# Feed-forward gate and up products by Strassen's algorithm in a hybrid encoder trunk on one Trainium2 core

## Chip, cores and metric

One core of one Trainium2 chip runs the whole step as one program. The metric is device time in microseconds from one launch; the number of a kernel is the median of its runs. The kernel before has 2403.69 us (three runs, 2400.80 to 2404.43).

## The reference, cut to what matters

The program computes two layers of a streaming encoder for 512 prompt tokens and 8 x 16 sample tokens, 640 columns in all, width 1024, in fp32. Each layer has a mixer (pooling and differential attention in layer 0, RWKV-7 in layer 1), a cross-attention and a SwiGLU feed-forward of width 2816. What the change touches is the last of these:

```python
D_FF = -(-8 * D_MODEL // (3 * 256)) * 256        # 2816 = 22 blocks of 128
def swiglu(h, wg, wu, wd):
    return (jax.nn.silu(h @ wg) * (h @ wu)) @ wd
...
        h = rmsnorm(x, P['norm_ffn_g'][l])
        x = x + swiglu(h, P['ffn_wg'][l], P['ffn_wu'][l], P['ffn_wd'][l])
```

## The kernel before, in words

Activations lie with features on the 128 partitions and the 640 tokens along the row; x is 8 such blocks. TensorE multiplies in a rounded fp32 format. To keep fp32 accuracy every operand is split (`split`, L216): the high part is a cast on ScalarE (L220), the low part the difference to it on VectorE (L211, or L214 when a scale is applied). A product is the sum of three: high by high, weight high by input low, weight low by input high. Weights come by `load_w` (L238): one DMA on SP's queue into `wr` (L245), a cast into `wh` on ScalarE (L247), a subtraction into `wl` on VectorE. `wtile` (L233) hands out two buffers each of wr, wh and wl in turn.

`block_steps` (L257) multiplies one block of 128 outputs: for each of the 8 blocks k of the inputs, the three products, each for two halves of 320 columns (`HALVES`), into two PSUM banks that take turns; 48 matmuls (L230) for a block of 1024 inputs. `gemm` (L274) strings such blocks together, with an evacuation function for each.

`ffn` (L1036), called once for each layer after `cross`, works so. `normed` (L523) multiplies x by the norm's gain and splits it into `xn`, without the row scale. `rms` (L484) works out the row scale: Square on ScalarE, the sum over the eight blocks in `acc` (GpSimd, the last one VectorE), a matmul with ones, root, reciprocal, a diagonal matrix, again a matmul with ones into `rstd`. Gate and up are computed in three groups of 8, 8 and 6 hidden blocks f. For each f the gate block is multiplied by rstd (VectorE) and goes through Silu (ScalarE); the up block is multiplied by rstd (VectorE), then by the gate (GpSimd), and split into `hid`. After each group the output projection adds 8 blocks to x (`add_x`, L530). Six PSUM banks serve these products in turn, two the norm. At the last group of layer 0, `mem_parts` transposes the memory prompt for the next layer through the banks of role r.

The order of instructions on each engine is worked out when the program is built: instructions are placed by their order in the program and by a simulated time at which they can run, so that later work may be placed ahead of earlier work that would still wait. On the chip every engine then keeps that order.

`cross` (L903) ends with a product of 8 blocks (24 matmuls each) that adds to x; `rwkv` (L1072) follows layer 0's feed-forward, `final` (L1895) layer 1's. SBUF holds 56 slots of 656 columns (`t`), 22 half slots of 256 (`n`, `NHALF`), and some wide tiles (zr0, zr1, bk0, bk1) that `rwkv` uses.

Of the kernel before, what the change touches and what calls it, by code (L numbers as in the profile page):

```python
# [9 lines left out]
F32 = mybir.dt.float32  # L10
F32R = mybir.dt.float32r
AF = mybir.ActivationFunctionType
ALU = mybir.AluOpType
# [8 lines left out]
NT = NP + NB * TS  # L22
NF = 22
HALVES = ((0, 320), (320, 320))
NEG = -1.0e30
EPS = 1e-6
NSLOT = 56
NHALF = 22
NSMALL = 32


# [8 lines left out]
class Trunk:  # L40
# [21 lines left out]
    def __init__(self, ctx, tc, io):  # L62
# [5 lines left out]
        self.dr = ctx.enter_context(tc.tile_pool(name="dr", bufs=1, space=DRAM))  # L68
        self.free = {"t": deque(range(NSLOT)), "n": deque(range(NHALF))}
        self.scopes = [{}]  # L70
# [54 lines left out]
    def take(self, k, name, kind="t", dt=F32):  # L125
        h = Held()
        h.slots = [(kind, self.pop(kind, name)) for _ in range(k)]
        h.extend(self.slot(kind, i, name, dt) for _, i in h.slots)
        return h
# [102 lines left out]

    def wtile(self, kind, dt):  # L233
        i = self.turn[kind]
        self.turn[kind] = (i + 1) % 2
        return self.wp.tile([128, 1024], dt, tag=f"{kind}{i}", name=kind, bufs=1)

    def load_w(self, src, kb, cols, rows=128):  # L238
# [795 lines left out]


    def ffn(self, l):  # L1036
        nc, io = self.nc, self.io
        self.banks(g=(0, 1, 2, 3, 4, 5), r=(6, 7))
        wg, wu, wd = io["ffn_wg"][l], io["ffn_wu"][l], io["ffn_wd"][l]
        hl = self.normed(self.col["norm_ffn_g"][:, 8 * l:8 * l + 8])  # L1040
        first = [[self.load_w(self.wview(w, 0, 8, 0, 128), 8, 128)] for w in (wg, wu)]
        _, rstd = self.rms("r")
        r0 = rstd[0]
        for f0, nf in ((0, 8), (8, 8), (16, 6)):
            hid = self.hl(nf, "hid")
            with self.scope():
                for f in range(nf):
                    g = self.t("gate")[:, 0:NT]
                    sg = self.t("sgate")[:, 0:NT]

                    def ev_g(m, pts):
                        for p, (t0, n) in zip(pts, HALVES):
                            self.tt(g[:, t0:t0 + n], p, r0[:, t0:t0 + n])
                            self.act(sg[:, t0:t0 + n], g[:, t0:t0 + n], AF.Silu)

                    def ev_u(m, pts):
                        for p, (t0, n) in zip(pts, HALVES):
                            self.tt(g[:, t0:t0 + n], p, r0[:, t0:t0 + n])
                            self.tt(g[:, t0:t0 + n], g[:, t0:t0 + n], sg[:, t0:t0 + n], eng=nc.gpsimd)
                            self.split((hid[f][0][:, t0:t0 + n], hid[f][1][:, t0:t0 + n]), g[:, t0:t0 + n])  # L1060

                    self.gemm(hl, wg, 128, ev_g, c0=(f0 + f) * 128, first=() if f0 + f else first[0])
                    self.gemm(hl, wu, 128, ev_u, c0=(f0 + f) * 128, first=() if f0 + f else first[1])
            if f0 == 16:
                self.give(hl, rstd)
                if l == 0:
                    self.mem = self.mem_parts("r")
            self.gemm(hid, wd, 1024, self.add_x, r0=f0 * 128)
            self.give(hid)


    def rwkv(self):  # L1072
# [898 lines left out]
```

## Time and profile before

| | |
|---|---|
| median of three runs | 2403.69 us (2400.80 to 2404.43) |
| profiled execution, its own time | 2400.51 us |
| its span, first to last instruction | 2398.7 us |
| TensorE busy | 2258.0 us (94%), 19213 matmuls, mean granted clock 0.967 |
| VectorE, ScalarE, GpSimd busy | 1257.2, 821.4, 448.3 us |
| DMA | 280.45 MB, mean 117 GB/s |

The span is the time between the first and the last instruction; the execution's own time is 1.8 us longer. Matmuls overlap, so the mean of one (310 ns) is longer than the distance from one to the next. A row of idle time names the engine whose event ended it. The granted clock is given as a share of 2.4 GHz; 0.5 is the lower level, 1.2 GHz.

### The profile page before, as it was taken

The numbers are of one execution on the slowest core, as the hardware profiler recorded it, in microseconds if no ns is written. First come the engines' busy times: TensorE is split into PE (matmuls) and PEld (weight loads), VectorE is DVE, ScalarE is ACT, GpSimd is POOL, SyncE is SP. The second block draws the span as 40 slices with busy tenths as digits, with TensorE's granted clock in tenths as the row PEclk, the third lists the DMA queues.
The fourth block names the chain that finished last, engine by engine and source line by source line (L and its number), as shares of the span: only waits on it lengthen the run. The fifth ranks groups of instructions, "written<-read, shape, count | busy, mean of one in ns | idle before, by whom it ended". The sixth has DMA issues, their size and how long they took to land. (4 is left out here: it accounts for less than half of the span.)

```text
span 2398.7 us, 46090 instructions
## 1 busy us (share of the span) xinstructions
PE 2258.0 (94%) x19213; PEld 2109.6 (88%) x19213; DVE 1257.2 (52%) x2193; ACT 821.4 (34%) x1521; POOL 448.3 (19%) x476
## 2 busy tenths in 40 slices
PE   8998899999999999989998976898999999999998
PEld 7886799879999999988887875676998899999997
DVE  3467434445433434485758885588534544244344
ACT  4335332334222212366745431222323432122122
POOL 1113220002101101245433111132100211021010
PEclk9999999999999999999998887898999999999998
DMA  3228545533222222353235666573444222222222
GB/s 118 75 71 304 155 136 158 172 93 89 80 71 80 71 85 74 112 171 107 83 111 160 164 166 165 165 223 111 145 128 154 69 76 72 80 71 80 80 73 77
DMA packets 428194, 280.45 MB, mean 117 GB/s; under 512 B 79001, under 2 KB 383406, under 8 KB 427985
## 3 DMA queue, kind: packets, MB, share of 16 engines
q1 hardware_dynamic: 424385, 268.01, 38.2%
q0 software_dynamic: 3600, 9.49, 1.1%
q8 instruction: 151, 2.47, 0.4%
q14 instruction: 58, 0.48, 0.1%
HBM read 231.22 MB, written 46.20 MB: 116 GB/s over the span
## 5 line engine op out<-in xcount | busy, mean ns | idle before, releaser
L230 PE MATMUL p_g<-xn,wh 128*128 128x320 f32 x3712 | 720.3, 310 | 0.4 <-ACT wh L247 0.4
L230 PEld LDWEIGHTS p_g<-xn,wh 128*128 128x128 f32 x3712 | 588.9, 188 | 9.6 <-issue 8.4
L247 ACT CAST wh<-wr 128x1024 fp32r<-128x1024 f32 (+3 forms) x287 | 274.4, 957 | 851.7 <-PE p_g L230 548.1
L230 PE MATMUL p_g<-xn,wl 128*128 128x320 f32 x1856 | 443.1, 310 | 3.6 <-DVE wl L211 3.6
L211 DVE TENSOR_TENSOR wl<-wr,wh 128x1024 fp32r<-128x1024 f32 (+2 forms) x259 | 307.3, 1186 | 71.6 <-ACT wh L247 59.6
L230 PEld LDWEIGHTS p_g<-xn,wl 128*128 128x128 f32 x1856 | 315.4, 188 | 7.5 <-DVE wl L211 4.0
L230 PE MATMUL p_g<-hid,wh 128*128 128x320 f32 x1408 | 264.4, 309 | 0.0
L211 POOL TENSOR_TENSOR gate<-gate,sgate 128x320 f32<-128x320 f32 x88 | 118.0, 1362 | 727.5 <-DVE gate L211 727.5
L211 DVE TENSOR_TENSOR gate<-p_g,rstd 128x320 f32<-128x320 f32 x176 | 78.4, 486 | 326.9 <-PE p_g L230 324.3
L211 DVE TENSOR_TENSOR x<-x,p_g 128x320 f32<-128x320 f32 x208 | 93.1, 484 | 266.4 <-PE p_g L230 266.3
L230 PEld LDWEIGHTS p_g<-hid,wh 128*128 128x128 f32 x1408 | 220.8, 188 | 0.0
L230 PE MATMUL p_g<-hid,wl 128*128 128x320 f32 x704 | 160.8, 309 | 0.0
L230 PE MATMUL p_g<-mixr,wh 128*128 128x320 f32 (+2 forms) x640 | 131.8, 317 | 5.9 <-ACT wh L247 1.8
L230 PEld LDWEIGHTS p_g<-hid,wl 128*128 128x128 f32 x704 | 117.8, 188 | 0.0
L230 PEld LDWEIGHTS p_g<-mixr,wh 128*128 128x128 f32 (+2 forms) x640 | 100.4, 182 | 15.8 <-issue 5.9
L230 PE MATMUL p_g<-xohl,wh 128*128 128x320 f32 x512 | 110.0, 319 | 3.7 <-ACT xohl L220 3.6
L230 PEld LDWEIGHTS p_g<-xohl,wh 128*128 128x128 f32 x512 | 82.3, 188 | 8.8 <-ACT xohl L220 5.9
L211 POOL TENSOR_TENSOR acc<-acc,sq 128x640 f32<-128x640 f32 x30 | 51.8, 1726 | 164.4 <-ACT sq L208 164.4
L230 PE MATMUL p_g<-mixr,wl 128*128 128x320 f32 (+2 forms) x320 | 79.2, 316 | 0.0
L211 POOL TENSOR_TENSOR wl<-wr,wh 128x1024 fp32r<-128x1024 f32 (+2 forms) x28 | 65.4, 2340 | 70.2 <-ACT wh L247 68.9
L211 DVE TENSOR_TENSOR hid<-gate,hid 128x320 fp32r<-128x320 f32 x88 | 71.5, 812 | 9.0 <-ACT hid L220 9.0
L972 POOL TENSOR_SCALAR xp<-xp,xsm 128x256 f32<-128x256 f32 x32 | 15.3, 478 | 311.6 <-DVE xsm L708 299.6
(491 smaller groups left out, 3719.5 us busy)
## 6 DMA issues: line engine op xcount, KB each, us to landing
wr<-in_ffn_wg SPq DMA_DIRECT2D x44, 512.0 KB
wr<-in_ffn_wu SPq DMA_DIRECT2D x44, 512.0 KB
kc<-in_cache_mem_k SPq DMA_DIRECT2D x64, 256.0 KB
vc<-in_cache_mem_v SPq DMA_DIRECT2D x64, 256.0 KB
wr<-in_ffn_wd SPq DMA_DIRECT2D x32, 512.0 KB
wr<-in_ev_w_in SPq DMA_DIRECT2D x16, 512.0 KB
wr<-in_xa_wk SPq DMA_DIRECT2D x16, 512.0 KB
vc<-in_cache_diff_v SPq DMA_DIRECT2D x32, 256.0 KB
```

Of the source, the lines that this page charges most:

```text
L211: (eng or self.nc.vector).tensor_tensor(out, a, b, op=op)
L230: self.nc.tensor.matmul(out, lhsT, rhs, start=start, stop=stop, **kw)
L247: nc.scalar.copy(wh[0:rows, 0:n], wr[0:rows, 0:n])
L972: nc.gpsimd.tensor_scalar(p, p, rs, 1.0, op0=ALU.mult, op1=ALU.mult)
```

## The change

Hidden blocks 0 to 3 of the 22 stay plain products; the other 18 are taken in nine pairs. For a pair (f, f+1) gate and up weights are cut into four parts: A11 and A12 are f by inputs 0 to 3 and 4 to 7, A21 and A22 the same of f+1; a tile holds the gate part in its first 512 columns and the up part in the other 512. The inputs are cut the same way into B11, B12, B21, B22 (inputs 0 to 3 or 4 to 7, columns 0 to 319 or 320 to 639). Strassen's algorithm (in Winograd's form) makes the 2 x 2 product with seven products of parts: four sums of weights (S1, S2, and in place A11-A21, A12-S2) on VectorE for each pair, four sums of inputs (T1 to T4) once a layer, and sums of the products in PSUM or by VectorE after ScalarE has copied a partial sum out.

For that the inputs are normalized before they are split: `rms` runs first, `ys` = x times gain times rstd, and `xn` is split from it. The product with rstd after the matmuls goes away, and Silu reads PSUM. The gate product moves from GpSimd to VectorE. The groups are of 4, 6, 6 and 6 blocks. `wh` and `wl` get three buffers, for all weight loads of the kernel; `NHALF` goes from 22 to 14 for their room. The raw weight parts lie in the four wide tiles and the two wr buffers and change places from pair to pair (`at`).

```diff
-NHALF = 22
+NHALF = 14
@@ wtile
-        self.turn[kind] = (i + 1) % 2
+        self.turn[kind] = (i + 1) % (2 if kind == "wr" else 3)
@@ ffn
-        hl = self.normed(self.col["norm_ffn_g"][:, 8 * l:8 * l + 8])
+        gcol = self.col["norm_ffn_g"][:, 8 * l:8 * l + 8]
         first = [[self.load_w(self.wview(w, 0, 8, 0, 128), 8, 128)] for w in (wg, wu)]
         _, rstd = self.rms("r")
-        r0 = rstd[0]
-        for f0, nf in ((0, 8), (8, 8), (16, 6)):
+        ys = self.blocks(8, "xf")
+        hl = self.hl(8, "xn")
+        for k in range(8):
+            self.stt(ys[k], self.x[k], gcol[:, k:k + 1], rstd[0])
+            self.split(hl[k], ys[k])
+        L, R = slice(0, 320), slice(320, 640)
+        c, d = self.hl(4, "xc"), self.hl(2, "xd")
+            hid = self.hl(4, "hid")
+            for f in range(4):
+                def ev_g(m, pts):
+                    for p, (t0, n) in zip(pts, HALVES):
+                        self.act(sg[:, t0:t0 + n], p, AF.Silu)
+                def ev_u(m, pts):
+                    for p, (t0, n) in zip(pts, HALVES):
+                        self.tt(pr[:, t0:t0 + n], p, sg[:, t0:t0 + n])
+                    self.split(hid[f], pr)
+                self.gemm(hl, wg, 128, ev_g, c0=f * 128, first=() if f else first[0])
+                self.gemm(hl, wu, 128, ev_u, c0=f * 128, first=() if f else first[1])
+                if f == 1:
+                    for k in range(4):
+                        y1, y2 = ys[k], ys[4 + k]
+                        self.tt(y1[:, L], y1[:, R], y1[:, L], ALU.subtract)
+                        self.tt(y1[:, R], y2[:, R], y1[:, R], ALU.subtract)
+                        self.tt(y2[:, R], y2[:, R], y1[:, L], ALU.subtract)
+                        self.tt(y2[:, L], y2[:, L], y2[:, R], ALU.subtract)
+                        self.split(c[k], y2)
+                        self.split([t[:, (L, R)[k % 2]] for t in d[k // 2]], y1[:, R])
+        for k in range(4):
+            self.split((hl[k][0][:, R], hl[k][1][:, R]), ys[k][:, L])
+        self.gemm(hid, wd, 1024, self.add_x)
...
+        for f0, nf in ((4, 6), (10, 6), (16, 6)):
+            self.banks(a=(0, 1, 2, 3), b=(4, 5, 6, 7), g=(4, 5, 6, 7), r=(6, 7))
+            hid = self.hl(nf, "hid")
+            at = dict(A11=0, A21=1, A22=2, A12=3, S1=4, S2=5)
+                for f in range(0, nf, 2):
+                    self.strassen(wg, wu, f0 + f, rhs, hid[f:f + 2], at)
+                    at = dict(A21=at["A11"], A22=at["S2"], A11=at["S1"], A12=at["A21"], S1=at["A12"], S2=at["A22"])
...
             self.gemm(hid, wd, 1024, self.add_x, r0=f0 * 128)
@@ strassen, new
+        for nm, fi, kh in (("A21", 1, 0), ("A22", 1, 1), ("A11", 0, 0), ("A12", 0, 1)):
+            A[nm] = raw(nm)
+            for i, w in enumerate((wg, wu)):
+                nc.sync.dma_start(out=A[nm][:, 512 * i:512 * i + 512].rearrange("p (k m) -> p k m", k=4),
+                                  in_=self.wview(w, 512 * kh, 4, (f + fi) * 128, 128))
+        def parts(t):
+            hi, lo = self.wtile("wh", F32R), self.wtile("wl", F32R)
+            self.split((hi, lo), t)
+            return [w.rearrange("p (i k m) -> p i k m", i=2, k=4) for w in (hi, lo)]
+        def product(pts, w, x, start):
+            for i, p in enumerate(pts):
+                n = 0
+                for k in range(4):
+                    for a, b in ((0, 0), (0, 1), (1, 0)):
+                        self.mm(p[:, 0:320], w[a][:, i, k, :], rhs[x][k][b], start=start and n == 0, stop=n == 11, skip_group_check=True)
+                        n += 1
+        def take(pts, i, s):
+            for p, t in zip(pts, tmp[i]):
+                nc.scalar.copy(t[:, s], p[:, 0:320])
+        def out(i, s, pts=None, direct=False):
+            tg, tu = [t[:, s] for t in tmp[i]]
+            if direct:
+                self.act(tg, pts[0][:, 0:320], AF.Silu)
+                self.tt(pr[i][:, s], pts[1][:, 0:320], tg)
+                return
+            self.tt(tg, tg, pts[0][:, 0:320], ALU.add)
+            self.act(tg, tg, AF.Silu)
+            self.tt(tu, tu, pts[1][:, 0:320], ALU.add)
+            self.tt(pr[i][:, s], tu, tg)
+        S1, S2 = raw("S1"), raw("S2")
+        self.tt(S1, A["A21"], A["A22"], ALU.add)
+        self.tt(S2, S1, A["A11"], ALU.subtract)
+        self.tt(A["A21"], A["A11"], A["A21"], ALU.subtract)
+        pa = [self.ps("a") for _ in range(2)]
+        product(pa, parts(A["A11"]), "B11", True)
+        take(pa, 0, L)
+        pb = [self.ps("b") for _ in range(2)]
+        product(pb, parts(A["A12"]), "B21", True)
+        out(0, L, pb)
+        product(pa, parts(S2), "T2", False)
+        take(pa, 1, L)
+        self.tt(A["A12"], A["A12"], S2, ALU.subtract)
+        product(pa, parts(S1), "T1", False)
+        take(pa, 1, R)
+        pc = [self.ps("b") for _ in range(2)]
+        product(pc, parts(A["A21"]), "T3", True)
+        out(1, R, pc)
+        product(pa, parts(A["A12"]), "B22", False)
+        out(0, R, pa, True)
+        self.split(hid[0], pr[0])
+        product(pc, parts(A["A22"]), "T4", False)
+        out(1, L, pc)
+        self.split(hid[1], pr[1])
```

## Rows read from the trace of the kernel before

**Rows 1.** The page's first part: busy time of each engine, its share of the span, and its instructions.

```profile
PE 2258.0 (94%) x19213; PEld 2109.6 (88%) x19213; DVE 1257.2 (52%) x2193; ACT 821.4 (34%) x1521; POOL 448.3 (19%) x476
```

**Rows 2.** The windows view over the feed-forward of layer 0 and of layer 1. Columns: the stretch, its length, busy time and instructions of PE, PEld, DVE, ACT and POOL, granted TensorE clock, busy share of DMA, GB/s.

```profile
560.35:1027.40 467.05, 467.05 (x3200) 466.69 (x3199) 190.03 (x261) 118.54 (x178) 70.55 (x59) 1.00 0.28 83
1914.74:2380.50 465.76, 465.76 (x3184) 465.44 (x3183) 186.16 (x252) 109.71 (x161) 60.07 (x45) 1.00 0.26 74
```

**Rows 3.** The same view over 130 us in the middle of layer 0's feed-forward.

```profile
645.00:775.00 130.00, 130.00 (x892) 130.00 (x891) 49.71 (x67) 28.63 (x40) 14.78 (x12) 1.00 0.25 74
```

**Rows 4.** The timeline of TensorE in a stretch of the memory-key product, which has one half of 256 columns, so that all its matmuls follow each other in one bank. Columns: start, length of the merged row in us, engine, line, operation, tiles, count.

```profile
1036.12 0.39 PE L230 MATMUL p_g<-memhl,wh 128*128 128x256 f32 x2
1036.36 0.28 PE L230 MATMUL p_g<-memhl,wl 128*128 128x256 f32 x1
1036.47 0.40 PE L230 MATMUL p_g<-memhl,wh 128*128 128x256 f32 x2
```

**Rows 5.** Groups of instructions by line and shape, over the whole span. Columns: line, engine, operation, tiles, shapes, count, then busy time in us and mean ns of one, then idle time of the engine before them and what ended it.

```profile
L230 PEld LDWEIGHTS p_g<-xn,wh 128*128 128x128 f32 x3712 | 588.9, 188 | 9.6 <-issue 8.4 <-ACT wh L247 0.5 <-DVE xq L214 0.2
...
L220 ACT CAST mixr<-mixt 128x640 fp32r<-128x640 f32 x40 | 28.7, 724 | 15.5 <-DVE mixt L214 15.4
```

**Rows 6.** The timeline of all engines at the start of layer 0's feed-forward.

```profile
560.35 0.75 PE L230 MATMUL p_g<-xn,wh 128*128 128x320 f32 x4
...
560.41 0.89 DVE L211 TENSOR_TENSOR x<-x,p_g 128x320 f32<-128x320 f32 x2 [0.50 <-PE p_g L230]
...
562.06 0.72 ACT L208 ACTIVATE sq<-x 128x640 f32<-128x640 f32 x1
...
562.53 0.88 DVE L214 SCALAR_TENSOR_TENSOR xn<-x,ct,xn 128x640 fp32r<-128x640 f32 x1
...
563.33 0.82 DVE L211 TENSOR_TENSOR acc<-acc,sq 128x640 f32<-128x640 f32 x1
...
567.21 1.17 PE L230 MATMUL p_r<-ones,acc 128*128 128x1 f32 x10
...
568.37 1.28 ACT L208 ACT_TABLE_LOAD   x1
...
569.67 0.27 ACT L208 ACTIVATE rtok<-p_r,epsc 128x5 f32<-128x5 f32 x1
...
569.97 0.19 DVE L512 RECIPROCAL rtok<-rtok 128x5 f32<-128x5 f32 x1
...
570.19 0.82 DVE L211 TENSOR_TENSOR dg<-ident,rtok 128x640 f32<-128x640 f32 x1
...
573.88 1.24 PE L230 MATMUL p_r<-dg,ones 128*128 128x320 f32 x4
...
574.62 0.49 DVE L200 COPY rstd<-p_r 128x320 f32<-128x320 f32 x1 [3.60 <-PE p_r L230]
...
575.16 0.43 ACT L198 COPY rstd<-p_r 128x320 f32<-128x320 f32 x1 [5.22 <-PE p_r L230]
```

**Rows 7.** Groups by line and shape in the stretch 568 to 1040 us.

```profile
L247 ACT CAST wh<-wr 128x1024 fp32r<-128x1024 f32 x63 | 66.3, 1053 | 275.0 <-PE p_g L230 167.5 <-issue 105.6 <-DVE dg L211 1.1
L211 POOL TENSOR_TENSOR gate<-gate,sgate 128x320 f32<-128x320 f32 x44 | 59.0, 1361 | 360.7 <-DVE gate L211 360.7
...
L211 DVE TENSOR_TENSOR gate<-p_g,rstd 128x320 f32<-128x320 f32 x88 | 39.2, 487 | 163.3 <-PE p_g L230 162.0 <-ACT sgate L208 1.3
...
L208 ACT ACTIVATE sgate<-gate 128x320 f32<-128x320 f32 x44 | 18.2, 462 | 0.0
```

**Rows 8.** The timeline of TensorE at the first product of the even layer, after an idle stretch: the first row after it, and the row that begins 12 matmuls later.

```profile
23.26 0.90 PE L230 MATMUL p_g<-xn,wl 128*128 128x320 f32 x2 [3.61 <-DVE wl L211]
...
26.62 0.58 PE L230 MATMUL p_g<-xn,wl 128*128 128x320 f32 x2
```

**Rows 9.** The timeline of VectorE in layer 0's feed-forward: a weight's low part without a gate product on GpSimd at the time, and one beside it.

```profile
640.63 1.23 DVE L211 TENSOR_TENSOR wl<-wr,wh 128x1024 fp32r<-128x1024 f32 x1
...
647.68 1.69 DVE L211 TENSOR_TENSOR wl<-wr,wh 128x1024 fp32r<-128x1024 f32 x1
```

**Rows 10.** The view of one tensor, the gate weights: time of a DMA issue on SP's queue in ns, least, median and most, and the first and last start in us.

```profile
L245 SPq DMA_DIRECT2D wr<-in_ffn_wg x44: 367/368/380, 551.4 to 2305.5; - x44
```

**Rows 11.** The windows view over three stretches of the RWKV layer (columns as in rows 2).

```profile
1100.00:1200.00 100.00, 99.27 (x621) 85.76 (x619) 61.04 (x77) 69.98 (x126) 49.45 (x36) 1.00 0.26 79
1300.00:1400.00 100.00, 91.94 (x1115) 84.07 (x1115) 83.44 (x164) 41.65 (x92) 19.49 (x30) 0.91 0.72 187
1600.00:1700.00 100.00, 89.73 (x1118) 76.93 (x1119) 72.06 (x132) 27.13 (x55) 25.57 (x24) 0.90 0.41 120
```

**Rows 12.** Groups by line and shape over the whole span, three of TensorE's with idle time before them.

```profile
L230 PE MATMUL p_g<-xn,wl 128*128 128x320 f32 x1856 | 443.1, 310 | 3.6 <-DVE wl L211 3.6
...
L230 PE MATMUL p_g<-wl,memhl 128*128 128x256 f32 x128 | 37.6, 294 | 4.9 <-DVE wl L211 4.9
...
L230 PE MATMUL p_l<-mT,gz 32*32 32x32 f32 x768 | 12.6, 213 | 12.8 <-DVE mT L1611 12.8
```

**Rows 13.** The timeline of TensorE after an idle stretch at the start of the RWKV layer.

```profile
1049.22 0.69 PE L227 MATMUL p_e<-ident,lastt 128*9 128x128 f32 x4 [3.44 <-DVE h L1121]
```

**Rows 14.** The windows view there (columns as in rows 2).

```profile
1045.00:1049.00 4.00, 0.78 (x7) 0.46 (x6) 4.00 (x16) 1.04 (x1) 2.87 (x6) 1.00 0.00 1
1049.00:1053.00 4.00, 3.73 (x28) 2.85 (x28) 4.00 (x9) 2.31 (x5) 2.32 (x5) 0.74 0.24 69
```

More of the change, by code (lines that the diff above doesn't have):

```diff
@@ new lines, in ffn @@
+        self.give(rstd)
+        L, R = slice(0, 320), slice(320, 640)
+        c, d = self.hl(4, "xc"), self.hl(2, "xd")
+        with self.scope():
+            hid = self.hl(4, "hid")
+            for f in range(4):
+                sg, pr = self.t("sgate")[:, 0:NT], self.t("gate")[:, 0:NT]
+                def ev_g(m, pts):
[16 more added lines that the diff above has]
+                        self.split([t[:, (L, R)[k % 2]] for t in d[k // 2]], y1[:, R])
@@ new lines, in ffn @@
+        for k in range(4):
+            self.split((hl[k][0][:, R], hl[k][1][:, R]), ys[k][:, L])
+        self.give(ys)
+        self.gemm(hid, wd, 1024, self.add_x)
+        self.give(hid)
+        part = lambda h, s: (h[0][:, s], h[1][:, s])
+        rhs = dict(B11=[part(hl[k], L) for k in range(4)], T1=[part(hl[k], R) for k in range(4)],
+                   B21=[part(hl[4 + k], L) for k in range(4)], B22=[part(hl[4 + k], R) for k in range(4)],
+                   T2=[part(c[k], R) for k in range(4)], T3=[part(d[k // 2], (L, R)[k % 2]) for k in range(4)],
+                   T4=[part(c[k], L) for k in range(4)])
@@ L1045, in ffn @@
+        for f0, nf in ((4, 6), (10, 6), (16, 6)):
+            self.banks(a=(0, 1, 2, 3), b=(4, 5, 6, 7), g=(4, 5, 6, 7), r=(6, 7))
             hid = self.hl(nf, "hid")
+            at = dict(A11=0, A21=1, A22=2, A12=3, S1=4, S2=5)
             with self.scope():
[L1047 to L1063, printed above, removed]
@@ L1064, in ffn @@
+                for f in range(0, nf, 2):
+                    self.strassen(wg, wu, f0 + f, rhs, hid[f:f + 2], at)
+                    at = dict(A21=at["A11"], A22=at["S2"], A11=at["S1"], A12=at["A21"], S1=at["A12"], S2=at["A22"])
             if f0 == 16:
-                self.give(hl, rstd)
+                self.give(hl, c, d)
                 if l == 0:
@@ L1069, in ffn, with strassen, raw @@
             self.give(hid)
+    def strassen(self, wg, wu, f, rhs, hid, at):
+        nc = self.nc
+        L, R = slice(0, 320), slice(320, 640)
+        def raw(nm):
+            i = at[nm]
+            if i < 4:
+                return self.wide(("zr0", "zr1", "bk0", "bk1")[i], "wraw")[:, 0:1024]
+            return self.wp.tile([128, 1024], F32, tag=f"wr{i - 4}", name="wraw", bufs=1)
+        A = {}
+        for nm, fi, kh in (("A21", 1, 0), ("A22", 1, 1), ("A11", 0, 0), ("A12", 0, 1)):
[27 more added lines that the diff above has]
+            self.tt(pr[i][:, s], tu, tg)
+        tmp = [[self.t(f"e{i}{j}", 1)[:, 0:NT] for j in range(2)] for i in range(2)]
+        pr = [self.t(f"gate{i}", 1)[:, 0:NT] for i in range(2)]
+        S1, S2 = raw("S1"), raw("S2")
[22 more added lines that the diff above has]
+        self.split(hid[1], pr[1])
```

## The prediction

> **What bounds the kernel now.** I read the engine totals first: TensorE is busy 2258.0 of 2398.7 us, VectorE 1257.2, ScalarE 821.4 [rows 1]. Then the stretch that the change rewrites. From the first feed-forward matmul (560.35) to the last (1027.40), and from 1914.74 to 2380.50 in layer 1, the windows show TensorE busy without a break, 467.05 and 465.76 us, at a granted clock of 1.00, while VectorE works 40% of the time [rows 2]. So in these 933 us only the number of matmuls and their pace count. Inside, 892 matmuls of 320 columns go by in 130.00 us [rows 3]: 145.7 ns each. DMA is at a quarter of its time there, 74 to 82 GB/s, so no weight is late.
>
> **Part 1, the products (removed: matmuls).** A pair of hidden blocks takes now 2 blocks x 2 matrices x 48 = 192 matmuls. By the new code it takes 7 products x 2 matrices x 4 k x 3 = 168, all of the same 320 columns. Blocks 0 to 3 of the 22 stay as they are; 9 pairs a layer change: 9 x 24 x 2 layers = 432 matmuls fewer, x 145.7 ns = **-62.9 us**, all of it on the path. The output projection keeps its 1056 matmuls a layer. One thing could spoil the pace: twelve matmuls in a row now go into one bank, where before two banks took turns. The memory-key product already does that: three matmuls of 256 columns start to start in 0.35 us (1036.12 to 1036.47), 117 ns each, that is 10 ns over 256 columns at 2.4 GHz; the old order has 12 ns over 320 columns [rows 3, 4]. The pace stays.
>
> Weight loads: each matmul has its own, mean 188 ns, and the loads' row is as full as the matmuls' (130.00 of 130.00 us) [rows 3, 5]; they overlap, since 188 ns would not fit into a pace of 145.7. The Trainium skill, page "TensorE: Matmul & The Clock Gate", section "The mechanism" (of its part on row and column tiling), says that a load overlaps a running matmul only where the row groups differ. By that rule each matmul removed here would give back its load too, 188 + 146 = 334 ns, and part 1 would be -144 us. The trace does not agree; the measurement decides.
>
> **Part 2, the start of each layer (moved: the norm).** Now the split of x into xn needs no row scale. The scale chain runs beside the first blocks, and TensorE goes from the cross-attention's last matmul into the first block without a gap (560.35). After the change every xn waits for rstd. The chain after that last matmul, with the durations of the rows [rows 6]: two adds into x 0.89; Square 0.72; add to acc 0.82 (VectorE); ten one-column matmuls 1.17; root 0.27 (its 1.28 us table load waits for nothing and fits beside acc); reciprocal 0.19; diagonal 0.82; four matmuls with ones 1.24; copy of the second half 0.49; scale-and-multiply 0.88; cast 0.72 [rows 5]. The sum is 8.2 us, and with some 0.05 us between steps 8.75: first matmul at 569.1. The 1.17 + 1.24 us of matmuls stand in the old stream as well, so the gap costs 6.3 net. Then VectorE feeds k by k: 0.88 + 0.82 = 1.70 us each, 13.6 us for eight. Gate and up blocks of f = 0 hold 96 matmuls, 14.0 us; if the order interleaves them by k, they eat the inputs as they come. After a gap TensorE starts at half clock: after an idle 3.61 us the next 12 matmuls took 3.36 us (280 ns each, the 1.2 GHz level), 1.6 us more than at 2.4 GHz [rows 8]. So 6.3 + 1.6 = 8 us per start. If block 0 runs alone first, it ends with the last split, 567.4 + 13.6 + 0.6 = 581.6, block 1 ends at 588.6, against 576.75 without a gap: 12 us. I take 8 (the old stream shows other matmuls placed inside a block, as at 567.21): **+16 us**, bounds 12.6 (no clock loss) and 24.
>
> What was queued behind: the removed evacuation multiplies (88 a layer, 0.486 us) and GpSimd's 44 gate products a layer (1.36 us mean) were off the path and give back nothing [rows 2, 7, 9]. Without GpSimd the VectorE subtractions lose their slow cases: 1.69 us beside a gate product, 1.23 without [rows 9].
>
> **Part 3, inside a pair (added: VectorE and ScalarE work, waits).** TensorE needs 168 x 145.7 ns = 24.5 us. VectorE: 7 low-part subtractions and 4 weight sums of 1024 columns at 1.23, 10 operations on 320 columns at 0.49, 2 low parts of 640 at 0.82: 13.5 + 4.9 + 1.6 = 20.0 us, a share of 82%. ScalarE: 7 casts x 1.05, 6 copies out of PSUM at 0.43, 4 Silu at 0.46, 2 casts of 640 at 0.72: 13.2 us [rows 5, 6, 7, 9]. SP issues 8 loads of 256 KB instead of 4 of 512 KB, the same bytes at some 0.37 us per issue [rows 10]; its queue holds the next pair's four parts in order, each until a tile of this pair is free (the last by product 5's split), and behind them only the next group's or the projection's loads, wanted 10 us later. The weight tiles wh and wl have three buffers, so a split may run two products (7 us) ahead of its use. New waits: product 4 (S1 with T1) accumulates straight after product 3 into the same banks and must wait for ScalarE's copies; the gate bank has the 1.75 us of the up half as cover, the copy takes 0.43, with one weight cast (1.05) ahead of it 1.5. It fits, barely; two casts ahead would not. VectorE's sums of PSUM parts wait for Silu, and the low-part subtractions queue behind them; TensorE waits two products later. No row has this mixture. The low end is 0, as the present stage and 1100 to 1200 (VectorE 61%, TensorE 99%) show; the high end is the RWKV stretches with VectorE at 72 and 83%, where TensorE is idle 8 to 10% [rows 2, 11]: 10% of 18 x 24.5 = 441 us is 44 us. These stretches are chains of small steps, the pair has 7 us of buffer, so I take a value near the low end, 1%: **+4.4 us**.
>
> **Part 4, handovers.** The first projection's last block ends in banks 0 and 1, which product 1 wants: two adds of 0.48 us, some 0.6 us a layer. In layer 0 the memory transposes now share banks 6 and 7 with the projection (before: 0 to 5 for it): 0 to 3 us, taken 1, since the projection can take blocks on banks 4 and 5 meanwhile. The combinations of xn halves (13 us of VectorE at f = 1, by 0.49 and 0.82 each) lie beside 56 us of plain blocks, and the T1 splits beside the first projection's 28 us. Sum **+2.2 us**.
>
> **Part 5, the rest of the kernel.** All weight loads get the third wh and wl; the 22 half slots shrink to 14. The waits of TensorE that a third buffer could shorten: 3.6 us on wl at the even layer, 4.9 at the memory products [rows 12]: at best -8.5. Fewer half slots mean earlier reuse in cross-attention and RWKV; the nearest row for such a late small tile is TensorE's 12.8 us behind mT [rows 12]. I take 0, bounds -8.5 and +13.
>
> **Sum.** -62.9 + 16 + 4.4 + 2.2 = -40.3 us on the profiled execution's 2400.51 gives 2360.2. That execution lies 3.2 below the median of the three runs (2403.69); I name **2362**.
>
> **Rivals.**
> (a) *Nearly no gain: VectorE sets the pace.* With 82% of its time taken and waits on Silu and casts between, a pair takes 27 us instead of 24.7, the upper bound of part 3. Against it: the buffers. For it: rows 11. Time 2360 + 40 = 2400. 8%.
> (b) *Slower: one gap per pair that also costs the clock.* Place: product 4 behind ScalarE's copies, or product 1 behind the last loads. At 1045.4 a gap of 3.44 us was followed by 4 us at a granted clock of 0.74 [rows 13, 14]: 3.44 + 4 x 0.26 = 4.5 us. Eighteen of them cost 81 us, less the 4 in the sum: 2437. It decides from 2.5 us a pair (44.7 over 18). The Trainium skill, same page, section "A second HAM failure mode: psum-queue depth-cycling", speaks against this change: a kernel that cycles its products through PSUM banks leaves TensorE idle between groups often enough that the clock swings between its levels. The present stage cycles six banks in 44 groups a layer and holds 1.00 [rows 2]; no run here shows it for products of twelve. 9%.
> (c) *More gain: interleaving hides the start and the third buffer pays.* 2400.5 - 62.9 + 12.6 - 5 = 2345. 7%.
> The forecast, 2350 to 2378 on its own, has 76%.
>
> **How the numbers follow.** The range 2346 to 2396 takes in the forecast, most of (c) and part of (a); (b) and the upper part of (a) are left out. A measurement of this kernel tells some 0.2% (5 us) from no change. Faster: 76 + 7 + half of (a) = 0.87. Same: the other half of (a), 0.04. Slower: (b), 0.09.
>
> **What would show it.** Feed-forward matmuls 6336 - 432 = 5904 at 146 ns; a gap of 8 to 9 us on TensorE at each start, ended by ScalarE's cast of xn; in the pairs a TensorE share of 99 to 100% at clock 1.00, VectorE near 82%. I am wrong if TensorE falls below 95% there, if the gap is 12 us or more, or if the stretches outside the feed-forward move by more than 8 us.

## The result and the profile after

The changed kernel took **2384.46 us**, the median of four runs (2375.11 to 2387.11), against 2403.34 for the kernel before on the same chip: a ratio of 0.9916, 95% interval 0.9888 to 0.9944. It is faster by 18.9 us, where I had forecast 41. The profiled execution has a span of 2383.0 us, 15.7 less than the one before.

The totals, in the form of [rows 1]; TensorE has 432 instructions fewer:

```profile
PE 2214.0 (93%) x18781; PEld 2062.5 (87%) x18781; DVE 1403.1 (59%) x2415; ACT 925.1 (39%) x1679; POOL 324.8 (14%) x388
```

The windows view by stage: feed-forward of layer 0 from the last cross-attention matmul on, what lies between, feed-forward of layer 1. The first and third answer to [rows 2].

```profile
561.60:1018.70 457.10, 444.22 (x2984) 441.35 (x2983) 270.83 (x379) 175.75 (x264) 13.97 (x17) 0.98 0.27 81
1018.70:1911.50 892.80, 797.39 (x8570) 708.38 (x8568) 580.03 (x1032) 364.65 (x722) 221.86 (x234) 0.91 0.52 143
1911.50:2363.30 451.80, 441.75 (x2968) 439.75 (x2967) 265.24 (x369) 166.45 (x246) 0.15 (x1) 0.98 0.24 71
```

The feed-forward stages shrank by 10.0 and 14.0 us, with 216 matmuls fewer in each (31.5 us). The stretch between them, 887.3 us before (1027.40 to 1914.74, [rows 2]), grew by 5.5. Unlike before, TensorE now has idle time in its feed-forward: length less busy time is 12.9 us in layer 0 and 10.1 in layer 1. And it has slow time: had the 31.5 us come off in full, the stages would be 435.6 and 434.3; busy time alone is 444.2 and 441.8. Both lie at the start, but for 1.7 us of idle time at the end of layer 0 (part 4 below). The timeline of TensorE at the start of layer 0 (compare [rows 6]):

```profile
561.31 0.46 PE L230 MATMUL p_g<-xohl,wl 128*128 128x320 f32 x2
565.72 2.29 PE L230 MATMUL p_r<-ones,acc 128*128 128x1 f32 x10 [3.96 <-DVE acc L211]
569.46 2.50 PE L230 MATMUL p_r<-dg,ones 128*128 128x320 f32 x4 [1.44 <-DVE dg L211]
574.15 1.97 PE L230 MATMUL p_g<-xn,wh 128*128 128x320 f32 x6 [2.19 <-ACT xn L220]
579.70 0.90 PE L230 MATMUL p_g<-xn,wh 128*128 128x320 f32 x2 [3.58 <-DVE xn L211]
...
585.20 0.50 PE L230 MATMUL p_g<-xn,wl 128*128 128x320 f32 x2
```

Then VectorE and ScalarE there, and the windows with the granted clock (the last column but two):

```profile
563.71 1.23 DVE L211 TENSOR_TENSOR wl<-wr,wh 128x1024 fp32r<-128x1024 f32 x1 [1.16 <-ACT wh L247]
564.85 0.82 DVE L211 TENSOR_TENSOR acc<-acc,sq 128x640 f32<-128x640 f32 x1
...
572.45 6.46 DVE L214 SCALAR_TENSOR_TENSOR xf<-x,ct,rstd 128x640 f32<-128x640 f32 x8 [1.03 <-ACT rstd L198]
578.83 5.23 DVE L211 TENSOR_TENSOR xn<-xf,xn 128x640 fp32r<-128x640 f32 x7
```

```profile
562.63 1.04 ACT L247 CAST wh<-wr 128x1024 fp32r<-128x1024 f32 x1 [2.12 <-DMA wr<-in_ffn_wg]
563.58 0.73 ACT L208 ACTIVATE sq<-x 128x640 f32<-128x640 f32 x1
```

```profile
561.60:565.70 4.10, 0.17 (x2) 0.00 (x0) 2.85 (x4) 2.97 (x3) 0.96 (x1) 0.89 0.49 140
565.70:574.10 8.40, 4.79 (x14) 3.38 (x14) 3.15 (x6) 1.42 (x3) 0.00 (x0) 0.50 0.22 62
574.10:579.70 5.60, 1.97 (x6) 1.57 (x6) 5.60 (x9) 5.08 (x7) 0.00 (x0) 0.50 0.00 0
579.70:585.00 5.30, 5.30 (x20) 5.30 (x21) 5.30 (x8) 0.00 (x0) 0.00 (x0) 0.50 0.01 3
585.00:590.00 5.00, 5.00 (x35) 5.00 (x35) 5.00 (x14) 1.67 (x4) 0.00 (x0) 0.97 0.00 0
```

Five things are to be seen. From the last cross-attention matmul (561.6) to the first product on xn (574.15) pass 12.55 us. The norm's own matmuls take 2.29 and 2.50 us where they took 1.17 and 1.24 in the running stream: the clock is granted at 0.50, the 1.2 GHz level, from 565.7 on (0.89 on average in the 4.1 us before). VectorE makes all eight scaled inputs xf in a row before the first low part, so TensorE, after six matmuls that need only high parts, waits 3.58 us more. And the half clock lasts until 585.2. A weight's cast, which starts only with the weight's transfer (2.12 us of idle time on ScalarE), and its low part stand ahead of the last Square and acc.

In layer 1 acc is ready sooner behind the last cross-attention matmul (1911.5), and the clock falls only behind the ones-product:

```profile
1914.53 1.28 PE L230 MATMUL p_r<-ones,acc 128*128 128x1 f32 x10 [2.84 <-DVE acc L211]
...
1921.93 1.97 PE L230 MATMUL p_g<-xn,wh 128*128 128x320 f32 x6 [2.19 <-ACT xn L220]
```

Behind the start the stage is as forecast. Windows over pairs in layer 0, the second of them two pairs long, and three groups of instructions of the pairs over the whole span:

```profile
665.00:736.00 71.00, 71.00 (x486) 71.00 (x486) 48.44 (x61) 34.77 (x53) 0.00 (x0) 1.00 0.31 90
```

```profile
675.00:724.50 49.50, 49.50 (x340) 49.50 (x340) 38.15 (x49) 25.51 (x39) 0.00 (x0) 1.00 0.29 83
```

```profile
L211 DVE TENSOR_TENSOR wl<-wraw,wh 128x1024 fp32r<-128x1024 f32 x126 | 154.1, 1223 | 107.9 <-ACT wh L220 92.4 <-PE p_b L230 13.8
L230 PEld LDWEIGHTS p_a<-xn,wh 128*128 128x128 f32 x864 | 144.4, 188 | 0.0
...
L1138 ACT COPY e<-p_a 128x320 f32<-128x320 f32 x108 | 45.7, 423 | 44.8 <-PE p_a L230 44.8
```

### The profile page after: what moved, and what is told of

It is laid out like the page before. It is cut to its first block, busy times and chain, and to the rows that moved or that the text cites. A ratio compares the mean times of both kernels' runs of the same rounds, so it can differ in the third digit from the quotient of the medians.

```text
span 2383.0 us, 45853 instructions
## 1 busy us (share of the span) xinstructions
PE 2214.0 (93%) x18781; PEld 2062.5 (87%) x18781; DVE 1403.1 (59%) x2415; ACT 925.1 (39%) x1679; POOL 324.8 (14%) x388
## 5 line engine op out<-in xcount | busy, mean ns | idle before, releaser
L230 PE MATMUL p_g<-xn,wh 128*128 128x320 f32 x1408 | 296.5, 319 | 12.2 <-DVE xn L211 7.2
L211 DVE TENSOR_TENSOR wl<-wr,wh 128x1024 fp32r<-128x1024 f32 (+2 forms) x203 | 202.0, 995 | 97.2 <-ACT wh L247 86.1
L230 PEld LDWEIGHTS p_g<-xn,wh 128*128 128x128 f32 x1408 | 233.0, 194 | 23.6 <-issue 8.4
L211 DVE TENSOR_TENSOR wl<-wraw,wh 128x1024 fp32r<-128x1024 f32 x126 | 154.1, 1223 | 107.9 <-ACT wh L220 92.4
L220 ACT CAST wh<-wraw 128x1024 fp32r<-128x1024 f32 x126 | 132.4, 1051 | 165.3 <-PE p_a L230 79.3
L230 PE MATMUL p_a<-xn,wh 128*128 128x320 f32 x864 | 191.5, 309 | 0.0
L230 PE MATMUL p_g<-xn,wl 128*128 128x320 f32 x704 | 183.8, 316 | 4.3 <-DVE wl L211 4.3
L230 PEld LDWEIGHTS p_a<-xn,wh 128*128 128x128 f32 x864 | 144.4, 188 | 0.0
L230 PE MATMUL p_a<-xn,wl 128*128 128x320 f32 x432 | 132.8, 309 | 0.0
L230 PEld LDWEIGHTS p_g<-xn,wl 128*128 128x128 f32 x704 | 125.6, 193 | 8.2 <-DVE wl L211 4.7
```

Of the source, the lines that this page charges most:

```text
L211: (eng or self.nc.vector).tensor_tensor(out, a, b, op=op)
L220: self.nc.scalar.copy(hi, src)
L230: self.nc.tensor.matmul(out, lhsT, rhs, start=start, stop=stop, **kw)
```

## The experiments

Each is compared with the kernel before on the same chip at the same time: 2401.82 us for the first four and 2406.62 for the next four, on one chip, and 2406.30 for the last three, on another. The diffs are shortened. "Stages" are the feed-forward of layer 0, the stretch between, and the feed-forward of layer 1, in the profiled execution; 467.1, 887.3, 465.8 in the kernel before, 457.1, 892.8, 451.8 after. A profile is one execution, and the totals of the kernel after alone range over 12 us (2375.11 to 2387.11); so a few us between two profiles count as a difference between builds only where the medians, or the waits and durations of the stage itself, show it too. My theory: the Strassen part gains what was forecast, and the norm at the start costs twice what I had put down. The rival: the norm costs what was put down, and the pairs or the other buffers eat the rest.

**The norm alone, on the kernel before (e1_norm_first).** All 22 blocks plain, two buffers, 22 half slots.

```diff
-        hl = self.normed(...)
+        for k in range(8):
+            self.stt(ys[k], self.x[k], gcol[:, k:k + 1], rstd[0])
+            self.split(hl[k], ys[k])
...
-  self.tt(g, p, r0); self.act(sg, g, AF.Silu)      # per half, gate
-  self.tt(g, p, r0); self.tt(g, g, sg, eng=nc.gpsimd)   # per half, up
+  self.act(sg, p, AF.Silu)
+  self.tt(g, p, sg)
```

> The kernel before with one part of the change alone: the norm runs first and xn is split from x times gain times rstd (the products with rstd after the matmuls go away). No Strassen, two weight buffers, 22 half slots. Theory START (each start costs some 15 us net, as the trace of after reads: 31.0 us for the first 96 matmuls in place of 14.0 + 2.4): 2403 + 2 x 15 = 2433. Rival, the forecast's own 8 us per start: 2419. Rival REST (the loss is outside the feed-forward): 2403 to 2410.

2448.94 us, ratio 1.0196 (1.0182 to 1.0209). The windows of its three stages:

```profile
562.50:1048.10 485.60, 474.97 (x3199) 472.97 (x3199) 156.05 (x232) 117.33 (x185) 10.73 (x15) 0.98 0.27 80
1048.10:1942.60 894.50, 800.58 (x8570) 707.81 (x8568) 580.60 (x1030) 365.28 (x720) 228.22 (x234) 0.92 0.50 140
1942.60:2425.60 483.00, 472.37 (x3184) 470.34 (x3183) 152.04 (x223) 109.03 (x168) 0.23 (x1) 0.98 0.24 71
```

The start costs 18.5 and 17.2 us, 35.7 together where START had 30, and the matmul count is that of before (one record is missing). Against these stages the kernel after is 59.7 us shorter in its feed-forward (28.5 and 31.2): that is the whole of the Strassen part with its waits and handovers, forecast as -62.9 + 4.4 + 2.2 = -56.3. The stretch between grew by 7.2 us although no buffer of it was changed.

**The change without the norm ahead of the matmuls (e2_plain_unscaled).** Blocks 0 to 3 multiply the unscaled split and are scaled behind the product, as before; the scaled inputs and their combinations are made beside them, and xn is split again before the first pair.

```diff
+        hl = self.normed(gcol)
...
-        for k in range(8):
-            self.stt(ys[k], self.x[k], gcol[:, k:k + 1], rstd[0])
-            self.split(hl[k], ys[k])
...
+  self.tt(pr, p, r0)           # behind gate and up of blocks 0 to 3
...
+        for k in range(8):      # behind block 3
+            self.split(hl[k], ys[k])
```

> The changed kernel with its start undone: blocks 0 to 3 use xn split without the row scale, as before (scale after the matmuls); the scaled copy is made beside them, and xn is split a second time from it after block 3, beside the first projection. START: the gap goes, 2384 - 2 x 14.6 = 2355. Rival, forecast's 8 us: 2368. If the second split is late at the first pair: 2360 or more. REST: 2380.

2345.21 us, ratio 0.9762 (0.9749 to 0.9775); stages 442.0, 884.4, 435.3. Its two feed-forward windows:

```profile
562.30:1004.30 442.00, 439.14 (x2984) 437.15 (x2984) 281.01 (x397) 177.29 (x264) 16.48 (x18) 1.00 0.30 87
...
1888.70:2324.00 435.30, 434.66 (x2967) 433.82 (x2967) 274.59 (x387) 166.90 (x246) 2.14 (x2) 1.00 0.26 77
```

Layer 1 is within 1.0 us of the ideal 434.3: the nine pairs cost next to no time beyond their matmuls. Layer 0 is 6.4 above its ideal, in part by a half clock at its start (last section).

**Buffers alone, on the kernel before (e3_buffers).** Three buffers of wh and wl, 14 half slots.

```diff
-NHALF = 22
+NHALF = 14
-        self.turn[kind] = (i + 1) % 2
+        self.turn[kind] = (i + 1) % (2 if kind == "wr" else 3)
```

> The kernel before with three buffers of wh and wl and 14 half slots, nothing else. REST (the 8 us by which the stretches outside the feed-forward grew come from slots and buffers): 2411. START: 2403, within 3.

2409.23 us, ratio 1.0036 (1.0020 to 1.0051); stages 470.7, 895.5, 466.1. The middle grew by 8.2 us, in an execution of 2414.13 us, 4.9 above the run's median; the medians differ by 7.4 in all. I took that for the price of the slots; the later runs show that it need not be.

**The order at the start (e4_order).** The kernel after, with VectorE told to scale input k only after the low part of input k - 2.

```diff
+  with self.tc.issue_after(subs[k - 2]):
       self.stt(ys[k], self.x[k], gcol[:, k:k + 1], rstd[0])
```

> The changed kernel with VectorE's order at the start written out: scale-and-multiply of block k comes after the low part of block k-2, in place of all eight first. If that order is the larger part of the 6.6 us per start beyond the forecast: the wait of 3.58 us goes and 2 x 4 to 5 us come back, 2375. Rival CLOCK (TensorE at half clock for 22 matmuls and for the norm's matmuls is the larger part): 2384, less 2 at most.

2373.31 us, ratio 0.9873 (0.9858 to 0.9888); stages 451.9, 891.7, 449.2: 5.2 and 2.6 us off the two starts. TensorE at the start of layer 0:

```profile
563.25 2.29 PE L230 MATMUL p_r<-ones,acc 128*128 128x1 f32 x10 [4.17 <-DVE acc L211]
566.99 2.50 PE L230 MATMUL p_r<-dg,ones 128*128 128x320 f32 x4 [1.44 <-DVE dg L211]
571.68 2.50 PE L230 MATMUL p_g<-xn,wh 128*128 128x320 f32 x8 [2.19 <-ACT xn L1055]
573.98 0.73 PE L230 MATMUL p_g<-xn,wl 128*128 128x320 f32 x2
```

The wait of 3.58 us is gone; the gap itself and the half clock in it stay. Layer 1 gained less because the wait for acc, 2.84 us in the kernel after, is longer there; again a weight's cast that had to await its transfer stands ahead of the Square:

```profile
1907.14 2.29 PE L230 MATMUL p_r<-ones,acc 128*128 128x1 f32 x10 [4.50 <-DVE acc L211]
```

**Work for TensorE in the gap (e5_warm).** e4 with float32 matmuls into a bank that nobody reads.

```diff
+  fill(self.x[6], 2); fill(self.x[7], 4)   # ahead of ones x acc
+  fill(acc, 2)                             # behind it
+  fill(dg, 3)                              # behind dg x ones
```

> The kernel after with VectorE's order at the start forced (e4_order, 2373 us) and, in the gap of the norm, idle-filling float32 matmuls of 320 columns on TensorE (identity times x[6] twice, x[7] four times, acc twice, dg three times), into a bank that nobody reads. CLOCK (the half clock at the start is what the idle gap costs beyond itself): the norm's own matmuls take 1.2 us each for 2.3 to 2.5 (-2.4 us), and the first 16 to 22 matmuls of a layer run at full clock (-2 to -2.7 us): 4 to 5 us a layer, so about 2364 us, and the granted clock of the gap reads near 1.00. Rival GAP ALONE (the clock is slow there for another reason, or the fillers stand in the chain's way): 2373 us or more.

2381.78 us, ratio 0.9902 (0.9886 to 0.9918), slower than e4; but the stages, 449.3, 902.8, 445.6, put that loss in the middle. At the start, windows and timeline:

```profile
558.60:568.20 9.60, 8.70 (x37) 5.58 (x35) 5.93 (x9) 4.38 (x6) 0.46 (x1) 1.00 0.38 111
568.20:573.20 5.00, 4.94 (x33) 4.82 (x34) 5.00 (x9) 2.19 (x4) 0.00 (x0) 1.00 0.00 0
```

```profile
562.01 1.27 PE L230 MATMUL p_r<-ones,acc 128*128 128x1 f32 x10
...
564.72 1.34 PE L230 MATMUL p_r<-dg,ones 128*128 128x320 f32 x4 [0.26 <-DVE dg L211]
```

The clock stays at 1.00, the norm's matmuls are back at 1.27 and 1.34 us, and the two feed-forward stages are 2.6 and 3.6 us shorter than e4's, although with only five banks left TensorE waits 1.7 us in each for ScalarE's sgate. Without that wait it would be 4.3 and 5.3. Not all of this is the clock: from the last cross-attention matmul to the ones-product pass 3.5 and 3.3 us here, 4.35 and 4.64 in e4, where acc came later. That leaves some 3.5 and 4.0 us for the half clock, a little less than the 4 to 5 expected. The total missed its 2364 mostly by the 11.1 us that the middle added; the kernel before, too, took 4.8 us more at that time.

**Buffers the other way (e6_two_buffers).** e2 with `NHALF = 22` and two buffers.

> e2_plain_unscaled (2345 us) with two buffers of wh and wl for three, and 22 half slots for 14: part 5 of the prediction taken back. REST (the buffers and slots cost the rest of the kernel what e3_buffers and the kernel after show, 5 to 8 us between the two feed-forward parts): 2338 us, with the stretch between the layers' feed-forward parts shorter than e2's 884.4 by up to 7 us. SPREAD (that stretch differs between builds by the execution alone): 2345 us; if the Strassen pairs need the third buffer, their waits on wl add 24 pair weights of 0.2 to 0.6 us, 5 to 14 us, so 2350 to 2359 us.

2360.59 us, ratio 0.9810 (0.9796 to 0.9824); stages 440.6, 903.1, 436.1. The pairs don't need the third buffer: the feed-forward stages are e2's within 1.4. And the middle, with the buffers of the kernel before, is the longest of all, 18.7 us above e2's; by the medians, each against the kernel before at its time, the whole kernel is some 11.5 us longer than e2. So the theory that buffers and slots stretch the middle falls.

**The kernel after again (e7_after_again).** Unchanged.

> The kernel after once more, unchanged: how far its stages differ from one profiled execution to another. SPREAD: the stretch between the feed-forward parts (892.8 us) and the stretch ahead of the first (561.6 us) differ from those by up to 5 us, so that the 5.5 us by which it is above the kernel before is no cost of the change. REST: 892 to 894 us again, 561 to 562 us again, and the total 2384 us within 3.

2383.06 us; stages 458.5, 892.0, 451.5. The middle repeats within 0.8 us, far closer than the 5 to 18 us by which builds differ; how far more executions would spread was not seen. The stretch ahead of the first feed-forward moved by 2.4 (559.2 for 561.6).

**One more pair for two plain blocks (e8_ten_pairs).** e2 with plain blocks 0 and 1 alone.

```diff
-            for f in range(4):
+            for f in range(2):
-        for f0, nf in ((4, 6), (10, 6), (16, 6)):
+        for f0, nf in ((2, 6), (8, 6), (14, 6), (20, 2)):
```

> e2_plain_unscaled (2345 us) with ten pairs for nine, and two plain blocks for four: a layer gains one pair, 24 matmuls of 0.146 us, 3.5 us; two layers 7 us. TENSORE SETS THE PACE: 2338 us. LATE SPLIT (the scaling and splitting of the streams, 14.7 us of VectorE, no longer fits beside two plain blocks of some 19.5 us in all with half the first projection's cover): TensorE waits at the first pair for 2 to 6 us a layer, 2342 to 2350 us.

2386.47 us, ratio 0.9913 (0.9898 to 0.9928); stages 455.2, 899.7, 445.3. LATE SPLIT, and larger than I had put it: instead of 3.5 us less, 13.2 and 10.0 more than e2 (the middle is 15.3 longer as well). Where, in layer 0, in a window and in TensorE's timeline:

```profile
590.00:605.00 15.00, 10.56 (x56) 9.93 (x55) 15.00 (x30) 9.05 (x17) 0.00 (x0) 0.83 0.03 9
```

```profile
597.40 0.56 PE L230 MATMUL p_g<-hid,wl 128*128 128x320 f32 x2 [1.97 <-DVE wl L211]
600.43 2.50 PE L230 MATMUL p_g<-hid,wh 128*128 128x320 f32 x8 [2.47 <-ACT hid L220]
```

VectorE is busy for the whole 15 us with the scaling and splitting, the projection's weights and hid queue behind it, and after the wait the eight matmuls run at half clock.

**The order of the RWKV part (e9_before_banks, e10_unscaled_banks, e11_after_banks).** The orders of TensorE, laid side by side, differ in the RWKV part, though its code is the same. In the trace of the kernel before the part has 6646 records of matmuls, from the first on mixr to the last on yo. With the longest common order left in place, 1084 of them stand elsewhere in the kernel after than before, 1138 in e1 and 1284 in e3; between the kernel after and its repeat e7 it is 3. So the theory ORDER: any edit ahead shifts the simulated times, the build orders the RWKV part anew, and that sets the middle. Three kernels got another set of banks in layer 0's last projection and nothing else: the kernel before four for six, e2 and the kernel after six for four.

```diff
                     self.mem = self.mem_parts("r")
+                    self.banks(g=(4, 5, 6, 7))                       # e9
+                    self.banks(g=(0, 1, 2, 3, 4, 5), r=(6, 7))       # e10, e11
```

> The kernel before with one thing changed: the last feed-forward projection of layer 0 takes the banks 4 to 7 for 0 to 5. Every engine has the same instructions; but the simulated times by which the order is worked out shift, and 925 of the 4420 matmuls between the start of the RWKV mixes and the end of the RWKV output projection come to stand elsewhere in TensorE's order. ORDER (what moved the rest of the kernel in the earlier runs is the order that the build gives the RWKV part, not buffers and slots): the stretch between the feed-forward parts leaves 887.3 us by 2 to 15 us, either way, and the total goes with it; the feed-forward stage stays at 467 within 1. REST (buffers and half slots cost it): 887 us within 1.5, total 2402 within 3.

> e2_plain_unscaled with the banks 0 to 5 for 4 to 7 in the last projection of layer 0: only 88 of the 4420 matmuls of the RWKV part stand elsewhere than in e2. ORDER: the stretch between the feed-forward parts is e2's 884.4 us within 2, so the total is e2's 2345 us, less the 1.7 us that the memory parts wait if more banks cover them: 2342 to 2346 us.

> The kernel after with the banks 0 to 5 for 4 to 7 in the last projection of layer 0: 1234 of the 4420 matmuls of the RWKV part stand elsewhere than in the kernel after. Buffers and slots are those of the kernel after. ORDER: the stretch between the feed-forward parts leaves 892.8 us by 2 to 12 us, either way; the feed-forward stage of layer 0 is 457 us, up to 1.7 less. REST: 892 to 894 us again, total 2383.

e9: 2413.82 us, ratio 1.0031 (1.0019 to 1.0043); stages 469.8, 894.6, 465.8. e10: **2343.03 us**, ratio 0.9740 (0.9723 to 0.9757), the lowest of all; stages 438.9, 886.4, 437.2. e11: 2388.87 us, ratio 0.9930 (0.9907 to 0.9952); stages 454.4, 900.6, 454.1. The middle moved by 7.3 and 7.8 us in e9 and e11, where many matmuls changed places (1133 and 1088 records by the same count), and by 2.0 in e10, where 119 did: ORDER. It is shown by e9, whose code, buffers and slots in that part are those of the kernel before: there the medians differ by 7.5. For e11 it rests on one trace each, since its ratio is not clear of that of the kernel after. And changed places need not cost: in e4 1070 records stand elsewhere than in the kernel after, and the middle is within 1.1 us. (The feed-forward of e9 also grew, by 2.7 where I had said 1; e11's shrank by 2.7 in layer 0, where I had said up to 1.7, and grew by 2.3 in layer 1, where acc came later.) The middle in three parts, first of the kernel before, then of e9:

```profile
1027.40:1270.00 242.60, 227.18 (x1537) 204.84 (x1536) 161.72 (x221) 146.82 (x260) 108.91 (x98) 0.97 0.39 114
1270.00:1730.00 460.00, 388.33 (x5618) 340.80 (x5616) 339.11 (x639) 162.39 (x345) 99.78 (x114) 0.87 0.60 163
1730.00:1914.70 184.70, 179.13 (x1420) 159.93 (x1420) 89.51 (x178) 61.12 (x124) 16.91 (x22) 1.00 0.40 123
```

```profile
1273.70:1741.00 467.30, 387.85 (x5611) 339.87 (x5610) 331.90 (x638) 161.75 (x344) 104.26 (x115) 0.87 0.59 160
```

With first and last part cut to equal lengths (their matmuls then agree within 2 and 8), all 7.3 us are in the 460 us of the recurrence. Its busy time is the same; TensorE waits longer. The list of waits there changes its head: mT 12.8 us in the kernel before; in e9 9.7 for a transfer of d_v and 8.6 for VectorE's gt. Which changed place costs most was not tried.

## Why the prediction was wrong, point by point

**Part 1 was right.** 3200 - 2984 and 3184 - 2968 are 216 matmuls a layer; twelve in one bank keep the pace (486 in 71.00 us, 146.1 ns). That the loads cost nothing extra is confirmed: they still take 188 ns each under that pace. By the rule of the Trainium skill, page "TensorE: Matmul & The Clock Gate", section "The mechanism", that a load overlaps a running matmul only where the row groups differ, the stages would have become 144 us shorter by the matmuls alone, as the prediction estimated; the Strassen part gave 59.7.

**Part 2 is the step that failed.** Its mechanism was right (a gap, behind the norm's chain, ended by ScalarE's cast of xn); its term, +16 us, is 35.7 by e1, above its upper bound of 24. The sum left out or mis-sized three things:
- *The order.* I took it that VectorE would scale and split input by input. The build put eight scalings first, so TensorE waited 3.58 us more per layer. e4 took that wait away and gave back 5.2 and 2.6 us.
- *The clock.* I counted the half clock from the first product on, 1.6 us [rows 8]. The rows show it from the norm's ones-product on in layer 0 (2.29 and 2.50 for 1.17 and 1.24 us), behind that product in layer 1, and in the first 26 and 28 products. e5 gave back 2.6 and 3.6 us net of a 1.7 us wait for a bank; some 3.5 and 4.0 us are the clock's own.
- *The neighbours of the chain.* A weight's cast (1.04) and low part (1.23) came to stand ahead of the last Square and acc; in layer 0 the cast also had to await the weight's transfer. I had summed the chain's own steps alone; the gap was 12.55 us in layer 0 (above the 12 that I had named as wrong) and 10.4 in layer 1 (1911.5 to 1921.93) against the 8.75 of the working. This share was not tested by itself.

Without its clock loss the term was 12.6 us. With 7.8 for the order and 7.5 for the clock that makes 27.9 of the 35.7; the other 7.8 no run splits up, and the neighbours are part of it.

**Part 3 was right in its mechanism, and smaller than put down.** TensorE is at 100% and clock 1.00 in the pairs, VectorE at 77% (38.15 of 49.50) against 82. The copies out of PSUM take 423 ns. e2's layer 1 leaves 1.0 us above the ideal for parts 3 and 4 together, where I had 2.2 + 0.6. Rival (a) falls with it. Rival (b) too: the Trainium skill, same page, section "A second HAM failure mode: psum-queue depth-cycling", tells of a kernel whose clock swings because TensorE idles briefly between its groups as they cycle through the banks. Here TensorE does not idle between them (71.00 of 71.00 us), and the clock stays at 1.00 through the pairs.

**Part 4.** The memory parts cost 0.92 + 0.79 us of waiting (I had 1); with six banks (e10, e11) these waits are gone.

**Part 5 is the second miss.** I took 0 and gave buffers and slots as bounds. The parts outside the feed-forward are 8.2 us longer in the profiled execution (1.2 ahead, 5.5 between, 1.5 behind), just above the 8 that I had named as too much. The 5.5 repeat with the same program (e7) and come with another order of the RWKV part: a bank set changed moves the middle by as much on both kernels (e9, e11), while the kernel with the buffers of before has the longest (e6). That the order is the cause in the kernel after is argued from these runs, not shown, since its buffers and slots changed too. The prediction had no such term. The 1.2 and 1.5 lie within what e7 moved by itself (2.4).

**The sum in the profiled executions:** -62.9 for the matmuls, +39.0 for the rest of the feed-forward (forecast 22.6) and +8.2 outside it (forecast 0) make -15.7, by which the spans differ. That the time lies between 2346 and 2396 is luck: the upper part of that range was there for rival (a), which did not come, and the norm's 35.7 lie above the bound of part 2. The sum also holds a slip of 1 us: 2360.2 and the 3.2 by which the profiled execution lay below the median make 2363.4, not 2362.

## What to carry to other kernels

A chain moved ahead of the engine that sets the pace costs its length in the order that the build gives its neighbours, and here the half clock in the gap as well as behind it; so keep the scale behind the products wherever the algebra permits, as e2 does, where 55.5 of the 62.9 us came through in the feed-forward. An edit ahead of a part that hangs on a planned order can move that part without touching it, here by up to 18 us (884.4 in e2, 902.8 in e5, with the same buffers): read the stages one by one, and try an edit that changes only the order before giving such a difference a cause.

## What the runs showed that was not expected

The clock fell beside very short waits. In e2, layer 0, TensorE idles for 0.61 and 0.51 us, the norm's ten one-column matmuls follow, and the products behind them run at the 1.2 GHz level for some 4 us (four in 1.13 us for 0.75). Whether the waits or the one-column matmuls did it was not tested by itself:

```profile
569.17 0.56 PE L230 MATMUL p_g<-xn,wh 128*128 128x320 f32 x2 [0.61 <-ACT xn L208]
570.24 0.56 PE L230 MATMUL p_g<-xn,wh 128*128 128x320 f32 x2 [0.51 <-DVE xn L214]
...
570.98 1.27 PE L230 MATMUL p_r<-ones,acc 128*128 128x1 f32 x10
...
572.34 1.13 PE L230 MATMUL p_g<-xn,wh 128*128 128x320 f32 x4
```

```profile
565.00:570.00 5.00, 4.12 (x27) 3.60 (x25) 5.00 (x6) 2.56 (x4) 1.58 (x1) 1.00 0.40 115
570.00:576.00 6.00, 5.73 (x29) 5.47 (x30) 3.07 (x5) 2.59 (x3) 0.00 (x0) 0.72 0.43 122
```

Other rows narrow it down. In the kernel before the same ten matmuls come without a wait, and the clock stays at 1.00 [rows 2, 6]. In e2's layer 1, with one wait of 0.61 us, it stays at 1.00 too; in e10's layer 0, with one wait of 0.84 us, it falls. First e2, then e10:

```profile
1895.89 0.56 PE L230 MATMUL p_g<-xn,wh 128*128 128x320 f32 x2 [0.61 <-DVE xn L214]
1896.00:1902.00 6.00, 5.97 (x42) 5.71 (x43) 2.72 (x4) 2.60 (x3) 0.00 (x0) 1.00 0.49 142
```

```profile
566.41 0.56 PE L230 MATMUL p_g<-xn,wh 128*128 128x320 f32 x2 [0.84 <-DVE xn L214]
570.00:576.00 6.00, 6.00 (x33) 5.84 (x33) 0.92 (x2) 0.00 (x0) 0.00 (x0) 0.78 0.30 87
```

And in e5 matmuls whose result nobody reads held the clock at 1.00 through a gap of 9.8 us and made the stage shorter.
